# Attention scores from one two-bank PSUM tile, value products of 256 columns, and transposes of two heads together

## The chip, the cores and the metric

The kernel runs on one core of one Trainium2 chip. The metric is the device time of one execution in microseconds; the time given for a kernel is the median of several runs. The profile is that of one further execution.

## The reference

The reference is a two-layer diffusion backbone with 256 latent tokens, 256 context tokens and a width of 1024. Each layer projects the modulated input once and splits the columns among three groups of heads, whose outputs are concatenated and projected back; a gated feed-forward network with a short convolution follows.

```python
h = _modulate(x, sa, ca); h_c = _modulate(ctx, sa_c, ca_c)
# A: 6 heads, two softmax maps each, 32 wide; keys and values: context + latent
p = softmax(q @ k.T * DA_SCALE);  p = p[:, :, 0] - lam * p[:, :, 1];  o_a = p @ v
# B: 6 heads, 64 wide; latent keys in a banded 2-D window with a position bias, and all context keys
s_win = where(in_band, q @ k_win.T * NA_SCALE + bias, NEG_INF)
p = softmax(concatenate([s_win, s_ctx]));  o_b = p @ concatenate([v_win, v_ctx])
# C: 4 heads, 96 wide; q, k and v from compressed projections (q_c, kv_c) and a shared rotary key
o_c = softmax(q @ k.T * MLA_SCALE) @ v
mix = concatenate([rmsnorm(o_a) * (1 - lam_init), o_b, o_c]) @ w_out
x = _post_norm(x, ga * mix, ...);  y = _conv_ffn(_modulate(x, sf, cf), ...);  x = _post_norm(x, gf * y, ...)
```

Context tokens go through the same layer, but attend to context alone; the last layer needs them only as keys and values. The output is the latent stream.

## The kernel before

**Products.** Weights and activations are split into a rounded part and a rest (`wsplit`, `split_from`: ScalarE casts, VectorE subtracts), and a product is three passes on TensorE (`mm3`, lines 134 to 136). All weights arrive by DMA in blocks of 512 KB on SP's queue.

**PSUM.** Its eight banks of 2 KB per partition are handed out by name: three `acc` (projections), one `ada`, two `sc` (scores) and two `tp` (transposes and value products).

**Attention.** Every head group is worked in pairs of heads `i`, in one or two streams (the latent queries against 512 keys, and in layer 0 the context queries against 256 keys), and in two query tiles `qt` of 128 rows per stream. For A, each head needs two score banks (its two maps); for B and C each of the two heads needs one. `score3` (line 626) writes the two banks of A and B with six products: for each of three passes, one product into each bank, from different rows of the array (`tile_position`). C's scores (line 831) are plain products of 96 rows.

`softmax_rows` then takes the row maximum on VectorE (line 381) and the exponential with its row sum on ScalarE (line 384). A combines its two maps on VectorE (lines 701 to 703); B first adds a bias that GpSimd has masked (lines 743 to 745); B and C scale by the reciprocal sum (line 674). `to_pT` transposes the probabilities on TensorE in blocks of 128 columns (line 392), and ScalarE copies them out (line 393). `pv` multiplies them with the values (line 400): for each block of keys and each head of the pair one product into a half of the partitions, 128 columns (one query tile) wide. The products are in full fp32, which TensorE runs as two instructions each. When both query tiles are done, `fin` normalises (A) and splits the result into `mix`.

`heads` traces this with delays: the lists `late[0]` and `late[1]` hold back the transposes and the value products, so that a head's transposes are traced after the next head's scores, and the value products one step later still.

**The order.** `ORDERS` lists, for each layer, the order in which projections (`aq0`, `bk1`, `v2`, ...), heads (`A0`, `B2`, `C1`) and early output products (`W3`) are traced. A planner then places each instruction on its engine's queue: it takes what is ready by its own estimate of time, and of several the one traced first. A tile of PSUM or SBUF with a limited number of buffers (`bufs`) is given out again once all accesses to the old one are over; its first writer waits for that. Each engine works through its queue in the order so fixed.

**Other users of the score banks.** In layer 0 the first value block is accumulated early in both `sc` banks (`evb`, line 493). `proj_vk` (from line 598) projects the second value block together with the rotary key, four token tiles of 288 columns, into `sc` banks, in the last layer two of the four into `acc`. Near the end of layer 0 the first projections of layer 1 are begun for the context tokens: two of them use `sc`, the compressed key and value (`early[14]`) and half of the first value block (`early["v"]`). The first is read until the compressed key is normalised (`rms_fm`, lines 755 to 770).

Of the kernel before, what the change touches and what calls it, by code (L numbers as in the profile page):

```python
# [8 lines left out]
F32 = mybir.dt.float32  # L9
# [68 lines left out]
def build(nc, tc, st, I, out):  # L78
    P = 128
# [23 lines left out]
    def scp():  # L103
        return bank("sc", 2)
# [283 lines left out]
    def to_pT(ap, p, nk):  # L388
        pT = ap.tile([P, 4, 128], F32, tag="pT", name="pT", bufs=4)
        pt = tpp()  # L390
        for kc in range(nk // P):
            T.transpose(pt[:, 128 * kc:128 * kc + 128], p[:, 128 * kc:128 * kc + 128], ident)  # L392
        S.copy(pT[:, 0:nk // P, :], pt[:, 0:nk].rearrange("p (k q) -> p k q", q=P))  # L393
        return pT

    def pv(po, qt, pTs, vt, c0, nk):
        n = nk // P
        for kc in range(n):
            for e in range(2):
                T.matmul(po[64 * e:64 * e + 64, 128 * qt:128 * qt + 128],  # L400
# [92 lines left out]
    evb = {pr: scp() for pr in (1, 0)}  # L493
# [42 lines left out]
    for l in range(L):  # L536
# [61 lines left out]
        def proj_vk():  # L598
            w = vkw
            for t in (2, 3, 0, 1):  # L600
                tok = slice(128 * t, 128 * t + 128)
                po = acc() if last and t % 2 else scp()
# [38 lines left out]
        def heads(i, sco, vv, c0, fin):  # L641
            for name, q0, nk in streams:
                box = {}
                for qt in range(2):
                    qs = slice(q0 - q0c + 128 * qt, q0 - q0c + 128 * qt + 128)
                    pTs = []

                    def finish(qt=qt, pTs=pTs, box=box, nk=nk, q0=q0):
                        if qt == 0:
                            box["po"] = tpp()  # L650
                        pv(box["po"], qt, pTs, vv, c0 + 128 * i, nk)
                        if qt == 1:
                            fin(box["po"][:, 0:256], slice(q0 - q0c, q0 - q0c + 256))

                    for e in range(2):
                        p = sco(2 * i + e, e, qs, qt, nk, name)

                        def transposed(p=p, e=e, pTs=pTs, nk=nk, finish=finish):
                            pTs.append(to_pT(ap, p, nk))
                            if e == 1:  # L660
                                late[1].append(finish)

                        late[0].append(transposed)
# [32 lines left out]
        def attn_a(i):  # L696
            def sco(h, e, qs, qt, nk, name):
                banks = [scp() for _ in range(2)]
# [17 lines left out]
            heads(i, sco, vt, 0, fin)  # L716
# [13 lines left out]
        def attn_b(i):  # L730
            banks = []

            def sco(h, e, qs, qt, nk, name):
                if e == 0:
                    banks[:] = [scp() for _ in range(2)]
# [92 lines left out]
        def attn_c(i):  # L828
            def sco(h, e, qs, qt, nk, name):
                sc = scp()  # L830
                T.matmul(sc[:, 0:nk], lhsT=mq[i][0:96, e, qs], rhs=mk[i][0:96, e, 0:nk], start=True, stop=True)  # L831
                return normed(sc, nk)
# [447 lines left out]
```

## Time and profile before

| | us |
|---|---|
| median of 3 runs (lowest to highest) | 1155.72 (1154.95 to 1156.66) |
| the profiled execution | 1158.58 |
| its span, first to last instruction | 1156.5 |

Busy time is the time in which an engine has at least one instruction under way, and a matmul's end is modelled. In rows in order of time, consecutive instructions of one line are merged into one row: start, duration, engine, line, operation, what is written and read, shape and count, and in brackets the idle time ahead and what ended it. A "visit" below is such a row of TensorE. In windows, the length comes first, then the busy time of each engine with the number of its instructions, the share of TensorE's full clock that was granted, and the share of the DMA engines.

### The profile page before, as it was taken

To read this page: it belongs to the slowest core of one execution; us is meant where nothing else is said; L and a number is where in the kernel's file an instruction comes from. 1 tells how busy PE (TensorE), PEld (TensorE's weight loads), DVE (VectorE), ACT (ScalarE), POOL (GpSimd) and SP (SyncE) were. 2 spreads that over 40 slices of the span, in tenths; PEclk is the share of its full clock that TensorE was granted. 3 is DMA by queue.
4 is the path that set the end of the run, shared out by engine and by line. 5 is a ranking of instruction groups with operands and counts; after the bars stand their busy time and mean duration, and the time that the engine had idled before them with its cause. 6 is when DMAs were issued, how large, how long until landed. Compare 5 with 4: busy or idle time off the path is not lost.

```text
span 1156.5 us, 17907 instructions
## 1 busy us (share of the span) xinstructions
PE 1107.0 (96%) x6776; PEld 902.1 (78%) x6776; DVE 836.1 (72%) x1505; ACT 591.2 (51%) x1063; POOL 83.8 (7%) x104
## 2 busy tenths in 40 slices
PE   5999999999998999999999999999999979999997
PEld 3877666686778888887888877897778758999985
DVE  4544677757588887986977687666766777888755
ACT  4345556656548644444352245555555656666541
POOL 0000100003123000000000002110000420000000
PEclk9999999999999999999999999998999988999999
DMA  9767112112143554643558894533111333555662
GB/s 362 295 241 279 58 37 74 37 37 86 51 164 97 197 169 144 199 152 116 186 174 309 311 328 131 176 94 99 53 55 56 128 132 121 183 183 188 201 203 89
DMA packets 58213, 179.19 MB, mean 155 GB/s; under 512 B 7024, under 2 KB 12432, under 8 KB 58128
## 3 DMA queue, kind: packets, MB, share of 16 engines
q1 hardware_dynamic: 58128, 178.05, 45.8%
q8 instruction: 54, 0.88, 0.3%
q14 instruction: 31, 0.25, 0.1%
HBM read 176.94 MB, written 1.08 MB: 154 GB/s over the span
## 4 chain that ended last, share of the span: by engine, by line
PE 85%; DVE 6%; ACT 2%; issue 2%; POOL 2%; DMA 2%; SPq 0%; DVEq 0%; POOLq 0%; ACTq 0%
PE acc L134 21%; PE acc L135 21%; PE acc L136 21%; PE sc L626 6%; PE tp L392 3%; PE tp L400 3%; PE sc L831 2%; DVE wlo L122 1%; PE sc L134 1%; PE sc L135 1%; PE sc L136 1%; POOL xn L344 1%; DMA rawr<-in_w_ada_e 1%; PE ada L234 1%; PE ada L136 1%
## 5 line engine op out<-in xcount | busy, mean ns | idle before, releaser
L121 ACT CAST whi<-raw 128x1024 fp32r<-128x1024 f32 (+3 forms) x204 | 212.0, 1043 | 248.7 <-PE acc L135 124.4
L122 DVE TENSOR_TENSOR wlo<-raw,whi 128x1024 fp32r<-128x1024 f32 (+3 forms) x204 | 248.4, 1221 | 121.4 <-ACT whi L121 117.1
L134 PE MATMUL acc<-hhi,whi 128*128 128x256 f32 (+1 forms) x960 | 327.3, 341 | 3.5 <-ACT hhi L360 3.5
L135 PE MATMUL acc<-hlo,whi 128*128 128x256 f32 (+1 forms) x960 | 325.4, 339 | 0.5 <-DVE hlo L361 0.3
L136 PE MATMUL acc<-hhi,wlo 128*128 128x256 f32 (+1 forms) x960 | 324.1, 338 | 0.4 <-DVE wlo L122 0.4
L134 PEld LDWEIGHTS acc<-hhi,whi 128*128 128x128 f32 x960 | 184.7, 193 | 28.2 <-issue 5.4
L135 PEld LDWEIGHTS acc<-hlo,whi 128*128 128x128 f32 x960 | 184.9, 193 | 22.2 <-issue 3.6
L136 PEld LDWEIGHTS acc<-hhi,wlo 128*128 128x128 f32 x960 | 184.6, 192 | 22.1 <-issue 3.8
L384 ACT ACTIVATE p<-sc,nm 128x512 f32<-128x512 f32 (+1 forms) x132 | 81.4, 619 | 26.0 <-DVE nm L381 24.5
L381 DVE TENSOR_REDUCE nm<-sc 128x1 f32<-128x512 f32 (+1 forms) x132 | 77.3, 598 | 22.7 <-PE sc L626 15.9
L393 ACT COPY pT<-tp 128x512 f32<-128x512 f32 (+1 forms) x96 | 49.4, 516 | 56.2 <-PE tp L392 55.8
L626 PE MATMUL sc<-stk,stq 32*128 32x512 f32 (+3 forms) x324 | 75.0, 392 | 1.0 <-ACT p L384 0.9
L626 PEld LDWEIGHTS sc<-stk,stq 32*128 32x128 f32 (+1 forms) x324 | 41.6, 183 | 26.4 <-issue 11.5
L1064 ACT ACTIVATE u<-acc,conv 128x256 f32<-128x256 f32 (+1 forms) x94 | 60.8, 647 | 1.4 <-PE acc L136 1.3
L1067 DVE SCALAR_TENSOR_TENSOR u<-acc,conv,u 128x255 f32<-128x255 f32 (+1 forms) x94 | 55.1, 586 | 6.3 <-ACT u L1064 6.3
L1068 DVE SCALAR_TENSOR_TENSOR u<-acc,conv,u 128x255 f32<-128x255 f32 (+1 forms) x94 | 55.4, 589 | 2.3
L215 DVE SCALAR_TENSOR_TENSOR ac<-raw,scT,ac 128x1024 f32<-128x1024 f32 x42 | 53.4, 1281 | 4.7 <-DMA raw<-in_w_ada 4.6
L392 PE MATMUL tp<-ident,p 128*128 128x128 f32 x320 | 52.6, 279 | 0.6 <-DVE p L674 0.5
L392 PEld LDWEIGHTS tp<-ident,p 128*128 128x128 f32 x320 | 36.8, 140 | 20.8 <-issue 8.5
L134 PE MATMUL acc<-whi,gBhi 128*128 128x512 f32 x133 | 52.0, 392 | 0.0
L135 PE MATMUL acc<-wlo,gBhi 128*128 128x512 f32 x133 | 51.9, 390 | 0.0
L136 PE MATMUL acc<-whi,gBlo 128*128 128x512 f32 x133 | 51.8, 391 | 0.0
(282 smaller groups left out, 1816.6 us busy)
## 6 DMA issues: line engine op xcount, KB each, us to landing
raw<-in_w_up SPq DMA_DIRECT2D x94, 512.0 KB
raw<-in_w_down SPq DMA_DIRECT2D x53, 512.0 KB
adalo<-in_w_ada SPq DMA_DIRECT2D x32, 512.0 KB
raw<-in_w_f SPq DMA_DIRECT2D x27, 512.0 KB
rawr<-in_w_ada SPq DMA_DIRECT2D x24, 512.0 KB
raw<-in_w_ada SPq DMA_DIRECT2D x24, 512.0 KB
raw<-in_w_out SPq DMA_DIRECT2D x16, 512.0 KB
rawr<-in_w_ada_e SPq DMA_DIRECT2D x12, 512.0 KB
```

The lines of the kernel that those rows point to most:

```text
L121: S.copy(hi, raw)
L122: V.tensor_tensor(lo, raw, hi.bitcast(F32), ALU.subtract)
L134: T.matmul(o, lhsT=lh, rhs=rh, start=first, stop=False)
L135: T.matmul(o, lhsT=lh, rhs=rl, start=False, stop=False)
L136: return T.matmul(o, lhsT=ll, rhs=rh, start=False, stop=last).ins
L381: V.reduce_max(nm, sc[:, 0:nk], axis=AX.X, negate=True)
L384: hT["exp"] = S.activation(p[:, 0:nk], sc[:, 0:nk], AF.Exp, bias=nm, accum_out=sums[:, 0:1]).ins
L392: T.transpose(pt[:, 128 * kc:128 * kc + 128], p[:, 128 * kc:128 * kc + 128], ident)
L626: T.matmul(sc[:, 0:nk], lhsT=q[r, a, qs], rhs=k[r, b, 0:nk], start=t == 0, stop=t == 2, tile_position=(r.start, 0))
L1064: S.activation(t, po[:, c], AF.Identity, scale=cw[:, 1:2], bias=cw[:, 3:4])
L1067: V.scalar_tensor_tensor(t3[:, :, 1:], p3[:, :, 0:255], cw[:, 0:1], t3[:, :, 1:], ALU.mult, ALU.add)
L1068: V.scalar_tensor_tensor(t3[:, :, 0:255], p3[:, :, 1:], cw[:, 2:3], t3[:, :, 0:255], ALU.mult, ALU.add)
```

## The change

There are three edits. First, `scp` gives out one tile of two banks (4 KB per partition, one buffer) instead of single banks with two buffers; A, B and C take both banks at once, and C issues the scores of both its heads together. `evb`, `proj_vk` and the early start of layer 1 take their banks in pairs too. Second, a stream's two query tiles share one pair of transposed tiles (`pT`, twice as wide), and `pv` runs once per stream with 256 columns. Third, for B and C the transposes of both heads of a query tile are traced together, head 1 first, and head 0's are queued behind head 1's. `out_early` first traces the value products that are still held back.

```diff
     def scp():
-        return bank("sc", 2)
+        t = ps.tile([P, 1024], F32, tag="sc", name="sc", bufs=1)
+        return [t[:, 0:512], t[:, 512:1024]]
...
-    def to_pT(ap, p, nk):
-        pT = ap.tile([P, 4, 128], F32, tag="pT", name="pT", bufs=4)
+    def to_pT(p, nk, pT, qt):
         pt = tpp()
         for kc in range(nk // P):
-            T.transpose(pt[:, 128 * kc:128 * kc + 128], p[:, 128 * kc:128 * kc + 128], ident)
-        S.copy(pT[:, 0:nk // P, :], pt[:, 0:nk].rearrange("p (k q) -> p k q", q=P))
-        return pT
-
-    def pv(po, qt, pTs, vt, c0, nk):
+            hT["tr"] = T.transpose(pt[:, 128 * kc:128 * kc + 128], p[:, 128 * kc:128 * kc + 128], ident).ins
+        S.copy(pT[:, 0:nk // P, 128 * qt:128 * qt + 128], pt[:, 0:nk].rearrange("p (k q) -> p k q", q=P))
+
+    def pv(po, pTs, vt, c0, nk):
...
-                T.matmul(po[64 * e:64 * e + 64, 128 * qt:128 * qt + 128],
+                T.matmul(po[64 * e:64 * e + 64, 0:256],
...
-    evb = {pr: scp() for pr in (1, 0)}
+    evb = dict(zip((1, 0), scp()))
...
         def proj_vk():
             w = vkw
+            pos = []
             for t in (2, 3, 0, 1):
                 tok = slice(128 * t, 128 * t + 128)
-                po = acc() if last and t % 2 else scp()
+                if not pos:
+                    pos = scp()
+                po = acc() if last and t % 2 else pos.pop(0)
...
-        def heads(i, sco, vv, c0, fin):
+        def heads(i, sco, vv, c0, fin, joint=True):
+            both = []
             for name, q0, nk in streams:
-                box = {}
+                pTs = [ap.tile([P, 4, 256], F32, tag="pT", name="pT", bufs=4) for _ in range(2)]
+
+                def finish(pTs=pTs, nk=nk, q0=q0):
+                    po = tpp()
+                    pv(po, pTs, vv, c0 + 128 * i, nk)
+                    fin(po[:, 0:256], slice(q0 - q0c, q0 - q0c + 256))
+
                 for qt in range(2):
...
-                        def transposed(p=p, e=e, pTs=pTs, nk=nk, finish=finish):
-                            pTs.append(to_pT(ap, p, nk))
-                            if e == 1:
+                        def transposed(ends=False, p=p, e=e, qt=qt, pTs=pTs, nk=nk, finish=finish):
+                            to_pT(p, nk, pTs[e], qt)
+                            if (ends or not joint and e == 1) and qt == 1:
                                 late[1].append(finish)
 
+                        if joint:
+                            both.append(transposed)
+                            if e == 0:
+                                continue
+
+                            def transposed(both=tuple(both)):
+                                both[1]()
+                                with tc.issue_after(hT["tr"]):
+                                    both[0](True)
+                            both.clear()
                         late[0].append(transposed)
...
-                banks = [scp() for _ in range(2)]
+                banks = scp()
                 score3(banks, aqs[i], aks[i], 32, 64 * e, qs, nk)
...
-            heads(i, sco, vt, 0, fin)
+            heads(i, sco, vt, 0, fin, False)
...
-                    banks[:] = [scp() for _ in range(2)]
+                    banks[:] = scp()
                     score3(banks, bqs[i], bks[i], 64, 0, qs, nk)
...
         def attn_c(i):
+            banks = []
+
             def sco(h, e, qs, qt, nk, name):
-                sc = scp()
-                T.matmul(sc[:, 0:nk], lhsT=mq[i][0:96, e, qs], rhs=mk[i][0:96, e, 0:nk], start=True, stop=True)
-                return normed(sc, nk)
+                if e == 0:
+                    banks[:] = scp()
+                    for n, sc in enumerate(banks):
+                        T.matmul(sc[:, 0:nk], lhsT=mq[i][0:96, n, qs], rhs=mk[i][0:96, n, 0:nk], start=True, stop=True)
+                return normed(banks[e], nk)
...
         def out_early(jb):
+            drain(1, 0)
...
+                e14, ev = scp()
...
-                    early[i] = (acc() if i < 14 else scp(), w, [(CTX, LO + HI)] if i == 14 else [])
+                    early[i] = (acc() if i < 14 else e14, w, [(CTX, LO + HI)] if i == 14 else [])
...
-                early["v"] = ({1: scp(), 0: acc()}, w, LO + HI, (0,))
+                early["v"] = ({1: ev, 0: acc()}, w, LO + HI, (0,))
```

## Rows read from the trace of the kernel before

**Rows 1.** The page: busy time by engine, and the last chain by engine.
```profile
PE 1107.0 (96%) x6776; PEld 902.1 (78%) x6776; DVE 836.1 (72%) x1505; ACT 591.2 (51%) x1063; POOL 83.8 (7%) x104
...
PE 85%; DVE 6%; ACT 2%; issue 2%; POOL 2%; DMA 2%; SPq 0%; DVEq 0%; POOLq 0%; ACTq 0%
```
**Rows 2.** The page, costliest groups: the score products (busy us, mean ns, idle before).
```profile
L626 PE MATMUL sc<-stk,stq 32*128 32x512 f32 (+3 forms) x324 | 75.0, 392 | 1.0 <-ACT p L384 0.9
```
**Rows 3.** Busy time by window: heads A, B of layer 0, A, B of layer 1.
```profile
159.30:248.30 89.00, 89.00 (x506) 60.54 (x506) 71.93 (x198) 57.55 (x153) 0.00 (x0) 1.00 0.15 48
261.80:316.50 54.70, 53.46 (x381) 37.98 (x380) 38.08 (x94) 32.41 (x86) 14.48 (x18) 1.00 0.23 71
824.90:895.40 70.50, 70.18 (x461) 54.67 (x460) 48.46 (x109) 39.07 (x86) 0.00 (x0) 1.00 0.16 55
895.40:938.00 42.60, 42.54 (x293) 30.79 (x292) 32.70 (x61) 27.73 (x53) 14.80 (x18) 1.00 0.40 127
sum 256.80, PE 255.19 PEld 183.99 DVE 191.17 ACT 156.76 POOL 29.28; mean PE 63.80 PEld 46.00 DVE 47.79 ACT 39.19 POOL 7.32
```
**Rows 4.** TensorE in order of time, within heads A of layer 0.
```profile
189.67 0.97 PE L626 MATMUL sc<-stk,stq 32*128 32x512 f32 x6
190.57 0.44 PE L392 MATMUL tp<-ident,p 128*128 128x128 f32 x2
...
196.72 0.96 PE L626 MATMUL sc<-stk,stq 32*128 32x512 f32 x3
...
199.36 0.50 PE L136 MATMUL acc<-hhi,wlo 128*128 128x512 f32 x1
199.70 0.39 PE L134 MATMUL acc<-hhi,whi 128*128 128x512 f32 x1
199.93 0.40 PE L135 MATMUL acc<-hlo,whi 128*128 128x512 f32 x1
200.25 0.96 PE L626 MATMUL sc<-stk,stq 32*128 32x512 f32 x3
```
**Rows 5.** TensorE in order of time: value products, narrow whole scores, transposes.
```profile
209.43 1.09 PE L400 MATMUL tp<-pT,vt 128*64 128x128 f32 x16
...
275.82 0.62 PE L626 MATMUL sc<-stk,stq 64*128 64x256 f32 x6
...
825.84 0.66 PE L392 MATMUL tp<-ident,p 128*128 128x128 f32 x4
826.43 1.97 PE L400 MATMUL tp<-pT,vm 128*64 128x128 f32 x32
```
**Rows 6.** Busy time of line 626 alone (PE, PEld), in the windows of rows 3.
```profile
159.30:248.30 89.00, 32.55 (x144) 19.07 (x144) 1.00 0.15 48
261.80:316.50 54.70, 14.12 (x72) 8.01 (x72) 1.00 0.23 71
824.90:895.40 70.50, 18.99 (x72) 9.85 (x72) 1.00 0.16 55
895.40:938.00 42.60, 9.35 (x36) 4.62 (x36) 1.00 0.40 127
```
**Rows 7.** Busy time of line 400 alone, the attention of both layers summed.
```profile
sum 350.30, PE 45.94 PEld 36.05; mean PE 22.97 PEld 18.03
```
**Rows 8.** All engines in order of time, one score group of heads A, layer 1.
```profile
844.38 0.96 PE L626 MATMUL sc<-stk,stq 32*128 32x512 f32 x6
...
845.35 1.23 DVE L122 TENSOR_TENSOR wlo<-raw,whi 128x1024 fp32r<-128x1024 f32 x1 [1.11 <-PE sc L626]
...
847.09 1.28 DVE L381 TENSOR_REDUCE nm<-sc 128x1 f32<-128x512 f32 x2
...
848.55 0.68 ACT L384 ACTIVATE p<-sc,nm 128x512 f32<-128x512 f32 x1
```
**Rows 9.** All engines in order of time, at the start of layer 1's attention.
```profile
762.19 0.30 PE L134 MATMUL sc<-whi,hhi 128*128 128x288 f32 x1
...
770.72 0.75 DVE L769 SCALAR_TENSOR_TENSOR cy<-sc,nrm,csq 128x512 f32<-128x512 f32 x1
```

More of the change, by code (lines that the diff above doesn't have):

```diff
@@ L639, in drain @@
                 late[n].pop(0)()
-        def heads(i, sco, vv, c0, fin):
+        def heads(i, sco, vv, c0, fin, joint=True):
+            both = []
             for name, q0, nk in streams:
-                box = {}
+                pTs = [ap.tile([P, 4, 256], F32, tag="pT", name="pT", bufs=4) for _ in range(2)]
[3 more added lines that the diff above has]
+                    fin(po[:, 0:256], slice(q0 - q0c, q0 - q0c + 256))
                 for qt in range(2):
                     qs = slice(q0 - q0c + 128 * qt, q0 - q0c + 128 * qt + 128)
[L646 to L653, printed above, removed]
                     for e in range(2):
                         p = sco(2 * i + e, e, qs, qt, nk, name)
-                        def transposed(p=p, e=e, pTs=pTs, nk=nk, finish=finish):
-                            pTs.append(to_pT(ap, p, nk))
-                            if e == 1:
+                        def transposed(ends=False, p=p, e=e, qt=qt, pTs=pTs, nk=nk, finish=finish):
+                            to_pT(p, nk, pTs[e], qt)
+                            if (ends or not joint and e == 1) and qt == 1:
                                 late[1].append(finish)
+                        if joint:
[7 more added lines that the diff above has]
+                            both.clear()
                         late[0].append(transposed)
```

## The prediction

> **What bounds the kernel now.** I read the first page, then busy time by stretch, then TensorE's rows in order of time. TensorE is busy 96% of the span and carries 85% of the chain that ended last; no other engine has a tenth of it [rows 1]. So time goes only where TensorE does less or waits less. The score products (line 626) hardly ever make it wait: 1.0 us of idle before 324 of them [rows 2]. Three stretches of attention in each layer matter: the differential heads A, the neighbourhood heads B, and the compressed heads C ahead of A. In A and B of both layers TensorE is busy 255.2 of 256.8 us while VectorE is at 191.2; in the longest, A of layer 0, VectorE has 71.9 of 89.0 us [rows 3]. The length of a stretch is thus TensorE's content, with VectorE next in line. Projections and output products, issued whenever they are ready, fill TensorE between scores.
>
> The rows in order of time show what those 256.8 us contain. A score group is six products: three passes for each of two banks. The two banks sit in different rows of the array, and where they are issued as pairs they run side by side: six products with 512 columns last 0.97 us. Where one bank comes free first its three go alone, and three alone last 0.96 us as well [rows 4]. A split group thus costs twice a whole one. And each visit to the score products has a price on its neighbours: a projection product is followed by the next after 0.23 us (199.70 to 199.93), after 0.34 when it is the first behind scores (199.36 to 199.70), and 0.32 pass from the last one to the scores (199.93 to 200.25) [rows 4]. That is 0.11 + 0.09 = 0.20 us per visit. I counted 88 visits for the 54 groups (36 of A, 18 of B): 42, 18, 18 and 10 in the four stretches; 22 of them hold all six products, 54 hold three, and some of the 22 are in the unpaired order.
>
> **The change part by part.**
>
> *Scores from one 4 KB tile.* Both banks come free at once, so the first product waits for both and the other five are ready with it; the order of tracing (pass by pass, bank by bank) then gives pairs. The 54 groups become 54 visits: 36 of 0.97 us (512 columns) and 18 of 0.62 (256 columns, [rows 5]) are 46.1 us against 75.0 now [rows 2]: 28.9 less. A row runs 0.07 us into the next one (0.97 against a spacing of 0.90), so 34 visits fewer take 2.4 off: 26.5. The neighbours give 34 x 0.20 = 6.8. By stretch from the group sums of line 626 [rows 6], with the same two corrections: A of layer 0, 32.55 - (12 x 0.97 + 12 x 0.62) = 13.5, net with 18 visits fewer 15.8; B of layer 0, 14.12 - 9.54 = 4.6, net 5.4; A of layer 1, 18.99 - 11.64 = 7.4, net 8.1; B of layer 1, 9.35 - 5.82 = 3.5, net 4.0. Together 33.3.
>
> *Value products of 256 columns.* 640 products of 128 columns become 320 of twice the width. The array streams as many columns as before, so only visits go: now 45.94 us [rows 7], in 41 visits by my count. A visit for both query tiles together already exists in layer 1 and lasts 1.97 us for 32 products; a visit of 16 lasts 1.09 [rows 5]. 16 latent visits and 8 context visits are 16 x 1.97 + 8 x 1.09 = 40.2, 5.7 less, of which 17 x 0.07 are overlap: 4.5. For the neighbours I take 0.15 (nearest row: 0.20 above, since these rows are shorter): 17 x 0.15 = 2.6. The output bank is no longer held from the first query tile to the second, so transposes have two banks more often; I take nothing for it, nor for the transposed tiles of twice the width, of which two pairs exist as before. Together 7.1: 1.5 in A and 2.0 in B of layer 0, nothing and 1.4 in layer 1, 2.2 in the C stretches.
>
> *Transposes of both heads together.* The number of products and of ScalarE's copies stays; they are in the same array mode as the projections, so alone they cost nothing more or less. Bounds: a gain of 0.20 us for each of 30 group visits joined, 6 us, or nothing; I take 0. They add a wait: the probability tile has two buffers, and both are now held until head 0's transposes, which come second. The next group's first exponential stands behind them on ScalarE, and copies and weight casts behind it. Four transposes take 0.59 us to the next row [rows 5], so the wait is at most about 1.2 us for 30 groups, 36 us. But the next scores, reduction and bias addition take that long too: I take 0 and keep the upper end for the range.
>
> *The chain of one group.* With one tile the next group starts after the second exponential. Reductions 1.28 us for two and the last exponential's 0.68, which starts 1.46 after them [rows 8], put the banks free 2.14 us after the reductions start; with 0.90 for the scores and 0.15 for the hand-over a cycle is 3.2 us. Now the same bank is scored again after 3.53 (196.72 to 200.25 [rows 4]). The lost double buffering is thus paid by the unsplit scores, if VectorE is prompt.
>
> *How much of it arrives.* TensorE could save 33.3 + 7.1 = 40.4 us; VectorE and the chain must follow. A of layer 0: 17.3 off 89.0 would leave VectorE 71.9 of 71.7, impossible; at a share of 90% the stretch is 80, and I take 9 (bounds 0 and 17.3). B of layer 0: 5.4 + 2.0 off 54.7 needs VectorE at 81%; 6.5. A of layer 1: 8.1 off 70.5, 78%; 7.5. B of layer 1: 5.4 off 42.6, 88%; 4.5. C: 2.2; 2. Sum 29.5.
>
> *One new wait.* At the start of layer 1 the two early accumulations, the compressed key's and the first value block's, now share the tile. The second value block (288 columns) took its first bank at 762.19, long before VectorE's last read of the compressed accumulation at 770.72 + 0.75 [rows 9]. Its tokens in score banks now wait until 771.5; queued behind it on TensorE are the rotary key's transposes, and C's first scores wait for those. Two of its four tokens still go to other banks, and the query projections fill in. Between 0 and 9.3 us; I take 2.5. The same pairing in layer 0 costs one copy (about 0.4), where transfers still fill the time: 0. The drained value products ahead of the output weights only order what had to come first: 0.
>
> Sum: 29.5 - 2.5 = 27 us less. The profiled execution took 1158.58 us (span 1156.5, 2.1 around it), 2.9 above the median of 1155.72; 27 off gives 1131.6 on its scale and **1129** as a median.
>
> **The rivals.**
>
> *Evacuation takes over (20%).* TensorE's saving in A is not used, because reductions, scalings and exponentials set the pace there: both A stretches stay, and B, C and the new wait give 6.5 + 4.5 + 2 - 2.5 = 10.5: 1145. For it: VectorE at 81% in A of layer 0, 71.9 of 89.0 us. Against it: 69% in A of layer 1 [rows 3], and the 13.5 us between A and B of layer 0 (248.3 to 261.8), outside the stretches with scores, into which weight splits can move. The Trainium skill's TensorEngine Tiling (Array Packing), section PSUM Bottleneck, says this in general: tiling speeds up TensorE but not the evacuation of PSUM, which may become the limit. By that rule the time would be this rival's; the trace agrees in layer 0 alone.
>
> *Groups are still cut (6%).* Earlier-traced projections turn ready within a group and go between its pairs; then mainly the value products gain, 7.1 - 2.5, about 5: 1151. Against it: the transposes and value products that cut groups now are traced after the scores that they cut.
>
> *Slower: the single tile stalls the chain (8%).* VectorE is in order, and a weight split (1.23 us) with other work can stand ahead of the reductions: at 847.09 they start 1.75 us after their scores end (844.38 + 0.96) [rows 8]. Such a cycle is 3.2 + 1.75 = 4.95 us, and no second bank covers it. If two in three of the 36 wide groups meet this, the mean is 4.4, 0.87 above today's 3.53, 31 us; where the chain decides, TensorE's saving is off the path, and the time is 1187. It decides from a mean cycle of about 3.6 us where TensorE has run out of filling work. Against it: of TensorE's 255.2 us in A and B only 75.0 are scores and under 46 values [rows 2, 3, 7], so over 130 are work that needs no score.
>
> **How the numbers follow.** My forecast has 66%, by itself between 1115 (all 40.4 arrive) and 1139. With the first rival most of the range from 1114 to 1147 is used; outside are the cut groups, the slower case and an unforeseen reordering. A measurement of this kernel can tell about 0.2%, 2.3 us, from no change. Faster: 66 + 20 + 5, less tails, 88%; same 4%; slower 8%.
>
> **What would show it.** Line 626 should stand in 54 visits of six with about 46 us in all; line 400 should have 320 products of 256 columns in 24 visits with some 40 us. A of layer 0 should take about 80 us with VectorE near 90%, and TensorE should idle a few us more there. At the start of layer 1 the 288-column products should pause until the compressed key is done. I am wrong if the stretch lengths stay while line 626 shrinks (evacuation), if visits stay above 70 (cut groups), or if TensorE idles more than 40 us in attention (stall).

## The result: slower by 2.8%, and the profile after

The changed kernel takes 1187.36 us (median of 4 runs, 1186.72 to 1191.55) against 1155.66 for the kernel before in the same series: a ratio of 1.0281, with a 95% interval from 1.0256 to 1.0307. The forecast was 1129, with a range to 1147. The profiled execution has a span of 1186.2 us against 1156.5, 29.7 more.

The page of the changed kernel answers to [rows 1] first: busy time by engine, and the last chain by engine.

```profile
PE 1094.6 (92%) x6456; PEld 880.8 (74%) x6456; DVE 835.2 (70%) x1505; ACT 589.7 (50%) x1063; POOL 83.0 (7%) x104
...
PE 76%; DVE 10%; ACT 7%; issue 3%; DMA 1%; POOL 1%; SPq 0%; DVEq 0%; POOLq 0%; ACTq 0%
```

TensorE works 12.4 us less than before (1107.0), as the change means it to; but it is idle for 1186.2 - 1094.6 = 91.6 us instead of 49.5. That is 42.1 more idle less 12.4 of work, the 29.7 us. The 12.4 hide a larger saving. The granted clock has two levels, 1.2 and 2.4 GHz; by a sum over the traces, 67.4 us of TensorE's work now fall at the lower one, against 19.6 before. A score product there takes up to 792 ns instead of 392, so half of the additional 47.8 us, 24 us, is my estimate of what the lower clock costs, and some 36 us of work are saved at equal clock. VectorE and ScalarE, 8% of the chain before, are now 17% of it. The costliest groups on the same page say where the idle time stands (busy us, mean ns, idle before, releaser); the first row answers to [rows 2].

```profile
L628 PE MATMUL sc<-stk,stq 32*128 32x512 f32 (+3 forms) x324 | 52.2, 426 | 27.2 <-ACT p L385 26.9
...
L392 PE MATMUL tp<-ident,p 128*128 128x128 f32 x320 | 54.7, 306 | 8.5 <-DVE p L714 6.5
...
L385 ACT ACTIVATE p<-sc,nm 128x512 f32<-128x512 f32 (+1 forms) x132 | 81.6, 619 | 60.7 <-DVE nm L382 55.1
...
L386 DVE RECIPROCAL sums<-sums 128x1 f32<-128x1 f32 x132 | 21.4, 162 | 82.5 <-ACT p L385 82.0
```

The score products fell from 75.0 to 52.2 us, and TensorE now waits 27.2 us ahead of them, where it waited 1.0; the releaser is the exponential (line 385). The reciprocal behind each exponential shows VectorE standing idle for it, 82.0 us.

Time is lost in one place. The next fence shows the score products of one layer by first and last start, first layer 0, then layer 1 (durations min/median/max, first and last start, shapes).

```profile
L628 PE MATMUL sc<-stk,stq x216: 269/392/792, 157.5 to 337.2; 32*128 32x512 f32 x36, 32*128 32x256 f32 x36, 64*128 64x512 f32 x18, 64*128 64x256 f32 x18
...
L628 PE MATMUL sc<-stk,stq x108: 383/393/792, 851.6 to 956.7; 32*128 32x512 f32 x72, 64*128 64x512 f32 x36
```

The same rows of the kernel before:

```profile
L626 PE MATMUL sc<-stk,stq x216: 269/384/521, 159.3 to 308.9; 32*128 32x512 f32 x36, 32*128 32x256 f32 x36, 64*128 64x512 f32 x18, 64*128 64x256 f32 x18
...
L626 PE MATMUL sc<-stk,stq x108: 384/392/502, 824.9 to 928.6; 32*128 32x512 f32 x72, 64*128 64x512 f32 x36
```

The last score of layer 0 is 28.3 us later than before (337.2 against 308.9), the last of layer 1 28.1 (956.7 against 928.6). So the attention of layer 0 loses all of it, and that of layer 1 comes out even. Busy time by window, as in [rows 3], splits layer 0 into the differential stretch A and the neighbourhood stretch B:

```profile
157.40:274.50 117.10, 104.47 (x579) 71.64 (x578) 78.18 (x200) 61.79 (x159) 0.00 (x0) 0.91 0.17 55
274.50:345.00 70.50, 51.94 (x276) 32.28 (x276) 35.71 (x97) 32.06 (x87) 13.82 (x18) 0.81 0.06 17
```

From the first scores of A to the first of B it was 102.5 us (159.3 to 261.8, the stretch A of [rows 3] and the work up to B), now it is 117.1; B was 54.7 and is 70.5. TensorE, idle for 1.2 us of the two before, is idle for 12.6 and 18.6. The two parts of A show when the projections and output products that fill it are used up:

```profile
157.40:237.00 79.60, 77.79 (x456) 55.59 (x455) 57.27 (x144) 43.98 (x110) 0.00 (x0) 1.00 0.23 73
237.00:274.50 37.50, 26.68 (x124) 16.05 (x123) 20.92 (x57) 17.82 (x49) 0.00 (x0) 0.71 0.05 15
```

Up to 237 us TensorE idles 1.8 us, from there to the end of A 10.8. With the idle time its granted clock falls from 1.00 to 0.91 in A and 0.81 in B, a mean between its two levels, and the rows there get longer: over the whole kernel the mean score product takes 426 ns instead of 392 [rows 2]. VectorE is at half load in B (35.7 of 70.5 us), so no engine is full there: a chain of waits sets the pace.

One wide group of A in the changed kernel shows the chain. All engines in order of time, other work left out:

```profile
163.07 0.97 PE L628 MATMUL sc<-stk,stq 32*128 32x512 f32 x6
...
164.54 0.68 DVE L382 TENSOR_REDUCE nm<-sc 128x1 f32<-128x512 f32 x1
...
165.44 0.58 ACT L393 COPY pT<-tp 128x512 f32<-128x512 f32 x1 [2.46 <-PE tp L392]
...
165.92 0.69 ACT L385 ACTIVATE p<-sc,nm 128x512 f32<-128x512 f32 x1
...
166.50 0.20 ACT L385 ACTIVATION_READ_ACCUMULATOR p<-sc,nm 128x1 f32 x1
...
166.74 0.16 DVE L386 RECIPROCAL sums<-sums 128x1 f32<-128x1 f32 x1 [1.51 <-ACT p L385]
166.81 0.67 DVE L382 TENSOR_REDUCE nm<-sc 128x1 f32<-128x512 f32 x1
166.83 1.05 ACT L122 CAST whi<-raw 128x1024 fp32r<-128x1024 f32 x1
...
167.78 0.68 ACT L385 ACTIVATE p<-sc,nm 128x512 f32<-128x512 f32 x1
...
168.78 0.96 PE L628 MATMUL sc<-stk,stq 32*128 32x512 f32 x6
```

Both banks are scored at 164.04. The second bank's reduction starts only at 166.81, behind the first bank's exponential and its reciprocal, although its input has been there for 2.8 us. That reciprocal stands ahead of the second reduction on VectorE in all 66 groups, by my count. ScalarE adds to the wait: a copy (165.44) goes ahead of the first exponential, and a weight cast of 1.05 us ahead of the second, which starts 0.30 us after its reduction has ended (167.48 to 167.78). The group takes 163.07 to 168.78, 5.7 us. In [rows 8] the two reductions stand in one row, back to back. I compared all 66 groups: in the kernel before the second reduction starts before the first exponential has ended in 56, in the changed kernel in none. This group stands early in A, where other work still fills TensorE; the same chain costs time once that work has run out.

### The profile page after: what moved, and what is told of

Same layout as the page of the kernel before. It is cut to its first block, busy times and chain, and to the rows that moved or that the text cites. A ratio compares the mean times of both kernels' runs of the same rounds, so it can differ in the third digit from the quotient of the medians.

```text
span 1186.2 us, 17233 instructions
## 1 busy us (share of the span) xinstructions
PE 1094.6 (92%) x6456; PEld 880.8 (74%) x6456; DVE 835.2 (70%) x1505; ACT 589.7 (50%) x1063; POOL 83.0 (7%) x104
## 4 chain that ended last, share of the span: by engine, by line
PE 76%; DVE 10%; ACT 7%; issue 3%; DMA 1%; POOL 1%; SPq 0%; DVEq 0%; POOLq 0%; ACTq 0%
PE acc L135 19%; PE acc L137 19%; PE acc L136 19%; PE tp L392 3%; PE tp L399 3%; ACT p L385 3%; PE sc L628 2%; DVE wlo L123 2%; PE sc L846 1%; PE sc L135 1%; DVE nm L382 1%; ACT whi L122 1%; PE sc L136 1%; PE sc L137 1%; ACT pT L393 1%
## 5 line engine op out<-in xcount | busy, mean ns | idle before, releaser
L135 PE MATMUL acc<-hhi,whi 128*128 128x256 f32 (+1 forms) x960 | 323.1, 337 | 4.0 <-ACT hhi L361 4.0
L386 DVE RECIPROCAL sums<-sums 128x1 f32<-128x1 f32 x132 | 21.4, 162 | 82.5 <-ACT p L385 82.0
L628 PE MATMUL sc<-stk,stq 32*128 32x512 f32 (+3 forms) x324 | 52.2, 426 | 27.2 <-ACT p L385 26.9
L628 PEld LDWEIGHTS sc<-stk,stq 32*128 32x128 f32 (+1 forms) x324 | 28.6, 209 | 49.3 <-ACT p L385 41.5
L392 PE MATMUL tp<-ident,p 128*128 128x128 f32 x320 | 54.7, 306 | 8.5 <-DVE p L714 6.5
L392 PEld LDWEIGHTS tp<-ident,p 128*128 128x128 f32 x320 | 39.9, 155 | 29.6 <-issue 16.7
```

What stands on the lines that cost most here:

```text
L135: T.matmul(o, lhsT=lh, rhs=rh, start=first, stop=False)
L392: hT["tr"] = T.transpose(pt[:, 128 * kc:128 * kc + 128], p[:, 128 * kc:128 * kc + 128], ident).ins
L628: T.matmul(sc[:, 0:nk], lhsT=q[r, a, qs], rhs=k[r, b, 0:nk], start=t == 0, stop=t == 2, tile_position=(r.start, 0))
```

## The experiments

Theory T1 is what that group shows: handed out as one tile, the two banks are treated as one object, and the second reduction keeps its place behind the first exponential. The rivals were T2 (the loss is that the next group must wait until both banks are free) and T3 (the joint transposes hold the probability buffers). T5 and T6 came later, on what is left when the order is mended: T5 says that it is the length of one group's chain, T6 that it lies in TensorE's own work or the order of its queue. Every time is a median, beside 1154 to 1156 for the kernel before in the same series.

**Two tiles in place of one** (everything else as changed).

```
     def scp():
-        t = ps.tile([P, 1024], F32, tag="sc", name="sc", bufs=1)
-        return [t[:, 0:512], t[:, 512:1024]]
+        return [bank("sc", 2) for _ in range(2)]
```

> The changed kernel with one edit: the scores helper hands out two tiles of one PSUM bank each, still taken together, in place of one tile of two banks. Everything else of the change stays (whole groups of six, 256-column value products, joint transposes). Theory T1 (the shared tile couples its banks: the second reduction is queued behind the first exponential, 66 of 66 groups): the second reduction again starts before the first exponential has ended in most groups, the cycle of a context group in the first A stage falls from about 5.5 us towards 4, and the time falls from 1187 to 1150 or below, as far as the other two edits gain what was forecast (1129). Rival T2 (the loss is that the next group must wait until both banks are free): both banks are still taken together, so the time stays at 1180 to 1190. Rival T3 (the joint transposes hold the buffers of the probabilities): stays at 1180 to 1190 too.

Measured: 1159.36 us (ratio 1.0042, 1.002 to 1.0063). Of 31.7 us lost, 27 are back with this one line, and the second reduction starts before the end of the first exponential in 51 of 66 groups. T3 alone is out, since the transposes are as they were. T2 isn't: for A and B the edit gives the banks out as in the kernel before, and with two tiles each bank is scored again as soon as it is free, as the next row shows, so this edit takes away the wait for both banks together with the order. But the gain did not come either: 1159, not 1150 or below. The row of the scores says why:

```profile
L627 PE MATMUL sc<-stk,stq 32*128 32x512 f32 (+3 forms) x324 | 80.3, 392 | 0.2
```

No wait, but 80.3 us of scores, more than the 75.0 before: with two tiles a bank that comes free first takes its three products alone (98 visits by my count, 15 of them of six). Whole groups came from the one tile, and so did the stall. From the start of the first reduction to the end of the second exponential a group takes 3.28 us on average here, 2.96 in the kernel before and 3.39 in the changed one, by my count; with two tiles that doesn't hold up TensorE, since a bank can be scored again before the other is free.

**Both reductions ahead of both exponentials** in the source, with the one tile kept.

```
-    (p0, s0), (p1, s1) = [softmax_rows(sc, nk, ap, f"p{m}") ...]
+    nms = [row_max(sc, nk) for sc in banks]
+    (p0, s0), (p1, s1) = [softmax_rows(sc, nk, ap, f"p{m}", nms[m]) ...]
```

(and the same in neighbourhood and compressed attention, there behind both bias additions).

> The changed kernel with its one tile of two banks, but in the source both row maxima (with the bias sums of neighbourhood attention ahead of them) stand before both exponentials. T1: the second reduction no longer queues behind the first exponential; instead the first exponential waits for the second reduction, some 0.5 us more than with two tiles; the chain is about 1.5 us shorter per group than in the changed kernel, so over 66 groups the time falls by 20 us or more, to 1145 to 1167. T2 and T3: the time stays at 1180 to 1190, since the tile and the joint transposes are as they were.

Measured: 1165.01 us (1.0086, 1.007 to 1.0103); 21 of the 31.7 us are back by the order alone. The next group still waits for both banks here, so T2 alone is out too; it can have a part in the 10 us that are left. The same place in its trace:

```profile
161.22 0.96 PE L632 MATMUL sc<-stk,stq 32*128 32x512 f32 x6
162.72 1.28 DVE L382 TENSOR_REDUCE nm<-sc 128x1 f32<-128x512 f32 x2
164.09 0.69 ACT L389 ACTIVATE p<-sc,nm 128x512 f32<-128x512 f32 x1
...
164.77 0.69 ACT L389 ACTIVATE p<-sc,nm 128x512 f32<-128x512 f32 x1
...
165.83 0.99 PE L632 MATMUL sc<-stk,stq 32*128 32x512 f32 x6
```

Reductions and exponentials now stand in pairs and a group takes 4.6 us. The one tile still couples the banks, the other way round: in 66 of 66 groups the first exponential starts after the second reduction has ended, though it needs only the first. So with one tile the operations of two engines on it ran in the order of the source in all 132 cases of these two kernels, although both only read it (in neighbourhood attention the bias is written first); with two tiles they did not. The Trainium skill's PSUM — Partial Sum Buffer, section PSUM bank collisions raise a hardware error, gives a reason for ordering reads at all: two engines must not access the same bank on the same partitions at once, reads included. Reduction and exponential of one group are on different banks, where that rule asks for no order, and two kernels with two tiles show them side by side: in 37 of 66 groups in this section's first run, and in 52 in the kernel before, the second reduction overlaps the first exponential. So the order here goes by tile and not by bank; that it is this protection which sets it is argued, no run shows it.

**Each edit alone or undone.**

```
 tile alone:    before + one tile of two banks, groups issued whole
 values alone:  before + value products of 256 columns
 no joint:      changed kernel with  def heads(..., joint=False)
 two tiles, no joint:  two tiles as above, with joint=False
```

> The kernel before with the first edit alone: groups issued whole into one tile of two banks (compressed attention's pairs too); value products stay at 128 columns and transposes stay single. T1: the whole loss is here, 1185 to 1200 (the changed kernel's 1187 plus what the other two edits gain). T3: the loss belongs to the joint transposes, so this one is at or below 1155: 1122 (33 us of weight waits gone) to 1155.

> The kernel before with the second edit alone: value products of 256 columns once per stream, transposes single, scores as before. The forecast's step: 7 us of visits and weight loads gone, so 1149 if all arrives. If the value products' later release (both query tiles needed) costs TensorE waits instead: 1155 to 1165. T1 says nothing here beyond that no 30 us loss appears.

> The changed kernel with the third edit alone undone: one tile of two banks and 256-column value products stay, neighbourhood and compressed attention transpose each head by itself again. T1 (the shared tile couples its banks): the joint transposes are a side matter, 1180 to 1195. T3 (the joint transposes hold two buffers of probabilities until both heads are done): most of the loss goes, 1155 to 1170.

> Two tiles of one bank taken together, 256-column value products, no joint transposes. Beside the kernel with two tiles and joint transposes (1159) it prices the third edit without the shared tile; beside the second edit alone (1170, runs from 1160 to 1174) it shows whether taking the two banks together matters by itself. If the joint transposes gain what the fewer visits suggest (20 fewer visits at about 0.2 us): 1162 to 1166; if they cost their wait: 1150 to 1157.

Measured: the tile alone 1192.57 (1.0327, 1.0311 to 1.0342); values alone 1169.89 (1.0144, 1.0117 to 1.0172; single runs from 1159.79 to 1174.33); no joint transposes 1194.92 (1.0357, 1.0337 to 1.0377); two tiles without joint transposes 1165.03 (1.0087, 1.0053 to 1.0121).

The whole loss is in the tile, as T1 says, and T3 has the wrong sign: joint transposes gain 0.8% with the one tile (1.0357 to 1.0281); with two the difference is 0.5%, but the intervals overlap (1.0087 and 1.0042), so it is not shown. The second edit by itself lost where 7 us of gain were forecast. Its value products did get shorter: by my count their visits go from 41 to 25, and the time from the start of each to the next product, summed, from 43.4 to 38.8 us. But with other run times the queue is planned anew, scores go out in 102 visits instead of 88, and TensorE's sum is unchanged, 1107.2 against 1107.0.

That its single runs lie so far apart goes with the clock: its four runs take 1159.79, 1168.68, 1171.10 and 1174.33 us at a mean granted clock of 0.989, 0.981, 0.979 and 0.974. The kernel with two tiles and no joint transposes has the same order of instructions on TensorE outside compressed attention, and its times follow the clock too (1159.61 us at 0.987 to 1171.52 at 0.977). Its trace was taken near the upper end: a span of 1169.1 us, against 1157.7 in the trace of the 256-column kernel. In it the clock fell at 876.9 us, for 17.1 us:

```profile
860.00:876.90 16.90, 16.80 (x98) 12.71 (x98) 10.84 (x20) 8.65 (x17) 0.00 (x0) 1.00 0.32 94
876.90:894.00 17.10, 17.10 (x57) 12.43 (x57) 9.75 (x25) 7.07 (x18) 0.00 (x0) 0.50 0.00 1
```

TensorE had been busy for 16.80 of the 16.9 us before. There was a second such fall at 187.4 us, for 6.8 us; the trace of the 256-column kernel has neither. Work at the lower level is 38.9 us in the one and 14.1 in the other; half the difference, 12.4 us by my estimate, is about the 11.4 between the spans. So the spread is the clock; why it falls there in one run and not in another stays open. The fastest runs of both still lie 5 to 6 us above the kernel before.

**Is the rest the chain?** T5 says that what keeps the mended kernel at 1165 is the length of one group's chain. Two kernels leave work out to shorten it without touching TensorE's work; one shortens the chain of the kernel before. All three also scale the scores down by 16, so that no exponential overflows, and their output is not the reference's. The edits in short:

```
 half maximum:  V.reduce_max(nm, sc[:, 0:256], ...)       # for 0:nk
 one maximum:   nms = [row_max(banks[0], nk)] * 2         # besides
```

> The kernel with one tile of two banks and both reductions ahead of the exponentials (1165), with each long reduction shortened: the row maximum is taken over the first 256 keys only, and all scores are scaled down by 16 so that no exponential overflows (the output is not the reference's). A reduction of 512 columns takes 0.684 us and one of 256 takes 0.417, so each of the 44 long pairs has 0.53 us less in its chain, 23 us in all; TensorE's work is the same. T5 (what is left over before is the chain of one group, with no second pair of banks to hide it): the time falls by 10 to 23 us, to 1142 to 1155. Rival T6 (what is left lies in TensorE's own work or in the order of its queue): within 4 us of 1165.

> The kernel before with the same shortening of the 88 long reductions (maximum over the first 256 keys, scores scaled down by 16; the output is not the reference's). In the attention stages of the kernel before TensorE is busy for 255 of 257 us, so the shorter chain should give nothing there: 1151 to 1156 (T5 and T6 alike). If it gains as much as in the kernel with one tile, then the chain bounds the kernel before too, and the reading of TensorE as its bound is wrong.

> The kernel with one tile, reductions first and the maximum over 256 keys (1151), cut further: one reduction serves both banks of a group, so the second reduction is left out (scores scaled down by 16, output not the reference's). It takes 0.42 us and two queue steps out of each of the 66 chains, some 28 to 35 us of chain; TensorE's work is unchanged. T5 (TensorE's saving is real and only the chain hides it): the time falls again by 8 to 20 us, to 1131 to 1143, towards the forecast 1129. T6 (the rest lies in TensorE's queue): within 4 us of 1151.

Measured: 1165 becomes 1151.06 (0.9971 of before, 0.9959 to 0.9983) and then 1136.22 (0.9838, 0.9818 to 0.9858), both within T5's bounds; the kernel before gets no faster, 1163.0 (1.0087, 1.0052 to 1.0122), slower than expected. So the chain bounds the kernels with one tile. For the kernel before, the run finds no gain, but it is no clean test: its queue was planned anew, with scores in 96 visits instead of 88 and value products in 48 instead of 41, by my count, and TensorE is busy 1111.6 us instead of 1107.0. That is about half of the 9 us that it loses. With the second reduction gone TensorE's saving is all there: busy 1075.8 us, 31.2 less than before, with 2.7 us of waits ahead of the scores.

**Can it be had with nothing left out?** One instruction for both maxima; one for both biases too; two tiles in neighbourhood attention only; these with one instruction for both maxima elsewhere; and two tiles whose groups are to be held together by order. The edits in short:

```
 one instruction: V.reduce_max(nm[P, 2], tile.rearrange("p (a c) -> p a c", a=2)[:, :, 0:nk])
 one bias:        V.tensor_tensor(both, both, bt[P, 2 x 256], ALU.add)
 hybrid:          one tile in A and C, two tiles in B (pool given back between)
 held groups:     two tiles; first product on bank 1, the other five issue_after it;
                  reductions and exponentials each issue_after the one before
```

> One tile of two banks, reductions first (1165), with both banks' row maxima taken by one instruction over the whole tile in place of two; nothing is left out. 512 columns take 0.684 us and 256 take 0.417, so 256 columns cost 0.267 and an instruction some 0.15 besides: the pair falls from 1.37 to about 1.22 us, and one queue step goes, 10 to 16 us of chain over 66 groups. T5 (the chain of one group sets the pace where nothing fills TensorE; the two cuts so far gave back 14 of 23 and 15 of 28 us): 1155 to 1160. T6 (the queue's order decides): within 3 us of 1165.

> As the kernel with one maximum instruction for both banks, and in neighbourhood attention both heads' bias tables are prepared as one tile and added to the two banks by one instruction (two of the three bias buffers are taken from differential attention's second probabilities). It takes another 0.15 to 0.3 us from each of 12 chains, 2 to 4 us: T5 expects 1152 to 1159, 1 to 3 us below the kernel without it. Rival: the larger bias tile arrives later (two transfers and GpSimd steps of twice the size ahead of one addition), and the group waits for it: 1160 or more.

> One tile of two banks with the reductions first in differential and compressed attention, two tiles of one bank in neighbourhood attention (the pool of the scores is given back and taken anew between them). In the kernel with one tile throughout and reductions first (1165), TensorE idles 17 of its 22 to 25 us in neighbourhood attention of layer 0, where nothing else is left to issue. T5: the idle time there falls by 8 us or more while differential attention keeps its groups of six, so 1148 to 1157. Rival T6: no gain, 1161 to 1168; or the work that fills TensorE runs out in differential attention in its place.

> One tile of two banks with one maximum instruction for both in differential and compressed attention, two tiles of one bank with separate maxima in neighbourhood attention. The two parts measured singly gave 2.9 us (two tiles in neighbourhood attention) and 6.7 us (one maximum) off 1165; neighbourhood attention no longer has the second, so T5 expects 1154 to 1159: at best level with the kernel before (1155). If the two parts shorten the same waits, 1158 to 1162.

> The kernel with two tiles taken together (1159: 98 visits of scores, 53 of them of three, since a half group goes out as soon as its own bank is free), with the group's first product put on the bank that is freed last and the others queued behind it, so that fewer groups are cut. T7 (with two tiles the saving of TensorE's time fails to appear because the groups are cut again; what is saved depends on the visits): visits of scores fall to about 75, TensorE's score time falls from 73.6 by some 7 us, and the time falls by 3 to 8 us, to 1151 to 1156. Rival: the queue's new order costs what the visits save, as in the other kernels with two tiles: 1158 to 1168.

Measured: one maximum instruction 1158.29 (1.0019, 1.0009 to 1.003), 6.7 us better as T5 had it; one bias addition 1160.94 (1.0044, 1.0027 to 1.0061), no better, in the rival's range, though its interval reaches T5's; the hybrid 1162.15 (1.0059, 1.0039 to 1.008), a gain of 2.9 us, as the rival T6 had it: TensorE's idle time in B of layer 0 falls from 14.9 to 7.0 us by my sum, as T5 wants, but B takes 57.1 us instead of 54.0; both together 1160.79 (1.0048, 1.0034 to 1.0063), in the range given for two parts that shorten the same waits; held groups 1156.52 (1.0001, 0.9988 to 1.0015), level with before. In the last the groups were not held: scores go out in 85 visits, 23 of them of six, where about 75 were expected. So no run here has whole groups on two tiles. None of these kernels beats the kernel before.

The row of the scores in six of these kernels, one fence each, shows the trade. Reductions first, half maximum, one maximum:

```profile
L632 PE MATMUL sc<-stk,stq 32*128 32x512 f32 (+3 forms) x324 | 48.4, 394 | 15.4 <-ACT p L389 15.3
```

```profile
L632 PE MATMUL sc<-stk,stq 32*128 32x512 f32 (+3 forms) x324 | 47.3, 390 | 8.2 <-ACT p L389 8.1
```

```profile
L632 PE MATMUL sc<-stk,stq 32*128 32x512 f32 (+3 forms) x324 | 47.8, 390 | 2.7 <-ACT p L389 2.6
```

One maximum instruction, then hybrid with it, then held groups:

```profile
L634 PE MATMUL sc<-stk,stq 32*128 32x512 f32 (+3 forms) x324 | 49.2, 402 | 10.8 <-ACT p L391 10.7
```

```profile
L654 PE MATMUL sc<-stk,stq 32*128 32x512 f32 (+3 forms) x324 | 58.3, 395 | 3.8 <-ACT p L411 3.6
```

```profile
L634 PE MATMUL sc<-stk,stq 32*128 32x512 f32 (+3 forms) x324 | 74.0, 391 | 0.2
```

With one tile the busy time is the 47 to 52 us of whole groups, and the wait shrinks with the chain: 27.2, 15.4, 10.8, 8.2, 2.7 us for times of 1187, 1165, 1158, 1151, 1136. From the start of the first reduction to the end of the second exponential the mean over the 66 groups is, by my count, 3.39, 2.66, 2.52, 2.33 and 1.93 us. Where two tiles take the wait away, the cut groups put back what it cost: hybrid 58.3 + 3.8 = 62.1 against 49.2 + 10.8 = 60.0.

**Is it only that the filling work ran out?** The kernel with one maximum instruction, with one block of layer 0's output products held back for B:

```
+            if jb == 3 and not last:
+                held.enter_context(tc.issue_after(hT["tr"]))
```

> The kernel with one tile and one maximum instruction (1158), with the first block of layer 0's output products (48 products, about 11 us of TensorE) held in TensorE's queue until neighbourhood attention, where TensorE idles 13 of 70 us; nothing else is changed. Theory F (the stall lies where the filling work runs out, and differential attention does not need that work): the idle time between 250 and 320 falls by 6 us or more and the time by 3 to 8 us, to 1150 to 1155. Rival T5 in its strict form (the chain sets the length of both stretches, and held work only moves the idle time into differential attention): the idle time from 160 to 320 stays within 3 us, and the time within 3 us of 1158.

(`held` is closed behind the block.) Measured: 1168.93 us (1.0116, 1.0101 to 1.0131). Both expectations fail. Busy time in A and B of layer 0, first without and then with the hold:

```profile
160.00:320.00 160.00, 144.32 (x832) 96.61 (x831) 108.56 (x254) 89.08 (x241) 14.16 (x18) 0.95 0.14 45
```

```profile
160.00:320.00 160.00, 134.66 (x760) 91.17 (x759) 105.71 (x243) 82.61 (x224) 13.89 (x18) 0.90 0.14 45
```

TensorE's idle time rose from 15.7 to 25.3 us. But the hold was too long to answer the question: the block waits for the last transpose traced ahead of it, which belongs to the second of B's three pairs of heads, and its products start at 301.3 us, in a stretch B that lasts from 261.3 to 322.3. With the hold, before and after that time:

```profile
261.30:301.30 40.00, 27.64 (x162) 16.56 (x162) 25.11 (x58) 19.71 (x57) 12.35 (x16) 0.83 0.09 27
301.30:322.30 21.00, 20.13 (x111) 14.80 (x109) 9.76 (x23) 8.30 (x21) 1.54 (x2) 1.00 0.11 32
```

TensorE idles 12.4 of the 40 us in which the block may not run, and 0.9 of the 21 in which other work is there to fill it. So filling work does hide the chain where it is at hand, and taking it away at the end of A lays the chain open there as well. What sets the size of the loss is both, the chain and the filling work; that shortening the chain alone gives time back is shown by the runs above.

## Why the prediction was wrong, step by step

*What bounds the kernel now* holds: shortening the chain of the kernel before gave nothing.

*Scores from one 4 KB tile* holds. 57 visits by my count, 51 of six, 52.2 us; in the kernel with one maximum, which works less at the lower clock (20.4 us by the same sum, not 67.4), they take 47.8 us (forecast 46). *Value products*: 24 visits as said, 39.8 us in that kernel (forecast 40.2). The forecast for TensorE's own work was 40.4 us less; 31.2 were measured there, and some 36 are in the changed kernel itself at equal clock, by the estimate above. So the saving was there, if smaller; the clock took 24 us of it back and the waits more than the rest.

*Transposes of both heads*, put at 0 with an upper end of 36 us lost, are a gain of about 8 us with the one tile (1194.92 to 1187.36).

*The chain of one group* is the step that failed. I took 2.14 us from the first reduction to the free banks by reading "reduce x2" and an exponential 1.46 us later off [rows 8]. That row comes from two tiles, where the first exponential runs beside the second reduction. I carried the overlap over to one tile, and did not ask whether the one tile permits it. It does not: the wide groups of A take 3.46 us on average in layer 0 and 3.51 in layer 1, by my count, and none is under 3.00. (The 3.39 above is the mean over all 66 groups, narrow ones too.) Even in the right order the wide groups of A take 2.86, since with one tile either the second reduction waits for the first exponential or the first exponential for the second reduction. The 2.14 was also close to the best case of the kernel before, whose wide groups of A take 2.71 and 2.98 on average. The cycle was put at 3.2 us; four wide groups at the head of A start at 157.49, 163.07, 168.78 and 173.78, 5.4 us apart.

*How much of it arrives* fails with it. I capped A by VectorE's load; the limit was the length of the chain, late in A and in B, where too little other work was left. A of layer 0, up to the first scores of B, became 14.6 us longer instead of 9 shorter, B 15.8 longer instead of 6.5 shorter. The sentence of the Trainium skill that I had for the first rival (TensorEngine Tiling (Array Packing), section PSUM Bottleneck) named the right side, evacuation, but as throughput: here VectorE was busy half of B.

*One new wait* at the start of layer 1 cost nothing visible: layer 0's last score is 28.3 us late, layer 1's first one 26.7 (851.6 against 824.9).

The rival on the slower side gave 1187, and 1187 came, by a neighbouring mechanism; that the number is the same is luck, and most of its terms differ. I had priced a weight split ahead of the reductions on VectorE, deciding from a cycle of about 3.6 us. What was right is that the chain decides where filling work runs out; the delay sits between the two exponentials, and the order meets every group, not two in three. With 8% it was priced too low, because the overlap was never questioned. My mark for a stall, more than 40 us idle in attention, was too coarse: TensorE idles 39.0 us in the attention of both layers (A, B and C), 31.2 of them in A and B of layer 0.

Open is why the kernels with two tiles, with hardly any waits ahead of the scores, lie 1 to 15 us above the kernel before even so, and why the hybrids, whose stall is almost gone, gain so little. The granted clock accounts for the spread within two of them; in all of them the queues are planned anew, and no run here separates that from the edits. Open is also how much of the 10 us that remain with one tile and the right order is the wait for both banks (T2): no kernel with whole groups on two tiles was measured.

## What to carry to other kernels

Before merging two buffers into one tile, list the operations of different engines that overlap between them, and take the chain of the merged tile from their sum in the order of the source. A saving on the busiest engine arrives only as long as the chain that feeds it stays shorter than the work that fills it. Where a tile has to be merged, group the operations by engine first (both reductions, then both exponentials) or make them one instruction: here that was worth 21 and then 7 us.

## What I had not expected of the hardware

One row maximum over two banks in one instruction took what was estimated from the single ones, 1.22 us against two of 0.684. In the kernel with it, by shape:

```profile
L383 DVE TENSOR_REDUCE nm<-sc 128x2 f32<-128x1024 f32 x44 | 53.7, 1220 | 6.7 <-PE sc L854 6.4
```

A stall came with a lower clock: in B of layer 0, where TensorE was busy 74% of the time, the granted clock was 0.81, against 1.00 at 98% before [rows 3]. But a stall is not needed for it: in the trace shown with the single edits the clock fell to its lower level with TensorE busy for 16.80 of the 16.9 us before. And six score products of 512 columns as pairs on two banks keep their 0.96 to 0.97 us at the full clock in the groups shown here: the saving that was forecast is real, 31 us in the kernel that can show it.
